# Residual, first norm, output projection and embedding gate with tokens on the partitions, and layer 1 begun by halves

## The chip, the cores and the metric

One of the eight cores of a Trainium2 chip runs the whole program. The time of a run is the time on the device in microseconds (us). Where a profile is quoted, it is one execution, recorded by the hardware profiler; its span reaches from the first to the last instruction.

## What is computed

Two layers of an encoder on 512 tokens of 1024 channels, all in float32. Each layer has a mixer and an MLP:

```python
for i in range(DEPTH):                                   # 2
    h = _mixer_sublayer(x, cos, sin, w_in[i], ...)       # two attentions, gated: (ga*ya + gb*yb) @ w_out
    x = _layer_norm(DEEPNORM_ALPHA * x + h, ln1_g[i], ln1_b[i])
    mlp = square(relu(x @ w_up[i])) @ w_down[i]          # 1024 -> 4096 -> 1024
    gate = sigmoid(x @ w_ple_gate[i] + b_ple_gate[i])
    ple = gate * (p[i] @ w_ple[i])                       # p[i]: 512 x 256
    x = _layer_norm(DEEPNORM_ALPHA * x + mlp + ple, ln2_g[i], ln2_b[i])
return x
```

## The kernel before, in words

**Number format.** Every operand of a matmul is split into a high part in TensorE's rounded float32 and a low part, the rest (`split`, L224: a cast on ScalarE (ACT), a subtraction on VectorE (DVE)). A product is then three matmuls: high x high, high x low, low x high (`mm3`, L269). The weights stand in memory in the order of use. `fetch` (L234) loads a set of eight 128x128 blocks (512 KB) by a DMA on SyncE's queue (SP), `prep` (L243) splits it, `ahead` and `weights` (L251, L262) keep a given number of sets in front of TensorE (PE); three buffers each for raw, high and low sets.

**Layout.** Channels lie on the partitions nearly everywhere: the activations are `X`, eight pairs of 128 channels by 512 tokens. A projection holds a block of weights still and streams 512 tokens past it. Only the MLP's second half (`Down`, L959) has tokens on the partitions; it uses a scheme of seven products in place of eight, with sums and differences of blocks.

**Order of a layer.** (1) The first projection `start` (keys, values, two queries; `linear_k_outer`, L283: four PSUM banks, input blocks in the outer loop), then attention, whose PE order is chosen by a small model (`Forecast`, L163), with gate projections as filling. (2) The second gates and branch projections give `M`, eight pairs (L1201 to L1215). (3) The residual `y` is put together as high + low of X on GpSimd (POOL, L1224). (4) The output projection goes block by block (`linear`), each block followed by `Norm.tile` (L854): residual added on DVE, squares on ACT, sums over blocks on POOL. Since the norm runs over partitions here, `begin` (L834) first subtracts an approximate mean (`shifted`, L824), and `finish` (L907) has TensorE make the sums over channels: 32 matmuls with one column (`moment`, L870), then statistics on DVE, then rows of mean and scale by transposes (`token_row`, L901). The embedding's matmuls (`ple_part`, L1177) fill in between. DVE and ACT then make the new X (`scaled`, L943, and L951) and the residual with bias. (5) The embedding gate: four blocks with k outer, four single ones; `embed` (L1237) adds gate times embedding to y. (6) The MLP. With its first two blocks the residual is turned to tokens on the partitions (`residual_turned`, L1250: 32 transposes on PE, copies on ACT). Four quarters, each with eight blocks `up` and seven products (`Down.product`, L1037; sums into y by `gather`, L1064). (7) The second norm, written out by hand for PE, DVE and ACT (L1328 on): batch statistics on DVE (`moments`, `statistics`), scaling (`scaled`, L1099), then `turned` (L1109) transposes back to channels in two halves of the tokens and applies scale and bias per channel. In layer 0 this gives the next X (`high`, `full`, `low`), with the next embedding half in between; then `start` of layer 1 follows. In layer 1 `store` (L1137) writes the transposed output in eight DMAs.

In a `manual_schedule` block the named engines keep the order of the text; elsewhere a planner sets the order of the engines.

Of the kernel before, what the change touches and what calls it, by code (L numbers as in the profile page):

```python
# [30 lines left out]
NEG = -3.0e38  # L31
LOOK = 2
# [10 lines left out]
def plan_layer(l):  # L43
# [35 lines left out]
    for t in range(KT):  # L79
        out.append(m_outer(("wo", t), "w_out", cols((t * P, P))))  # L80

    def ple(l, hh):
        return (("ple", l, hh), [("w_ple", l, [full[k]], cols(((hh * 4 + m) * P, P)))
                                 for m in range(4) for k in range(2)])

    if l == 0:
        out.append(ple(l, 0))
    out.append(ple(l, 1))
    gates = [cols((t * P, P)) for t in range(KT)]
    out += k_outer("pg0", "w_ple_gate", gates[:4])  # L90
    for t in range(4, KT):
        out.append(m_outer(("pg", t), "w_ple_gate", gates[t]))
# [108 lines left out]
def build(nc, tc, plan, down, xT, pT, wst, vec, sink, cst, outT):  # L201
# [3 lines left out]
    with ctx:  # L205
# [10 lines left out]
        rgap = rg.tile([P, 80], F32, name="rgap")  # L216
        nc.gpsimd.memset(rgap, 0.0)
        onec = cp.tile([P, 1], F32, name="onec")
        wgap = wp.tile([P, 96], F32, name="wgap", bufs=1)
        nc.gpsimd.memset(wgap, 0.0)  # L220
        nc.vector.memset(onec, 1.0 / D)
# [5 lines left out]


        offs = np.cumsum([0] + [len(t) * P * P for _, t in plan + down])
        down_at = {key: int(offs[len(plan) + n]) for n, (key, _) in enumerate(down)}  # L230
        ready, fetched = {}, {}
# [11 lines left out]
        def prep(c):  # L243
            st, n, cut = fetched.pop(c)
            hi = wp.tile([P, 1024], F32R, tag="whi", name=f"whi{c}")
            lo = wp.tile([P, 1024], F32R, tag="wlo", name=f"wlo{c}")
            for a in range(0, n, cut):
                split(hi[:, a:a + cut], lo[:, a:a + cut], st[:, a:a + cut])
            ready[c] = (hi, lo)
# [19 lines left out]
        def mm3(ps, w, i, x, start, stop):  # L269
            s = slice(i * P, (i + 1) * P)  # L270
            nc.tensor.matmul(ps, w[0][:, s], x[0], start=start, stop=False)  # L271
            nc.tensor.matmul(ps, w[0][:, s], x[1], start=False, stop=False)  # L272
            nc.tensor.matmul(ps, w[1][:, s], x[0], start=False, stop=stop)  # L273
# [20 lines left out]


# [13 lines left out]
        def attention_block(l, av, rp, vt, OA, OB):  # L309
# [371 lines left out]
            kps, vps, q0, q1 = linear_k_outer(l, "start", X, load_constants)  # L681
# [127 lines left out]
        class Norm:  # L809
            def __init__(self, mp, y, alpha, name):  # L810
                self.mp, self.y, self.alpha, self.name = mp, y, alpha, name

            def add(self, out, ps, y):
                if self.alpha == 1.0:
                    nc.vector.tensor_tensor(out, ps, y, ALU.add)
                else:
                    nc.vector.scalar_tensor_tensor(out, y, self.alpha, ps, ALU.mult, ALU.add)

            def shift(self, ps):
                zr = self.mp.tile([P, S], F32R, tag="zr", name="zr" + self.name, bufs=1)  # L820
                self.add(zr, ps, self.y[0])
                return zr

            def shifted(self, zr):  # L824
                ones_r = self.mp.tile([P, P], F32R, tag="ones", name="ones" + self.name, bufs=1)
                nc.vector.memset(ones_r.bitcast(F32), 1.0 / P)
                cb = bank("o", "cb" + self.name)
                nc.tensor.matmul(cb, ones_r, zr, start=True, stop=True)
                cs = self.mp.tile([P, S], F32, tag="shift", name="cs" + self.name, bufs=1)
                nc.scalar.activation(cs, cb, AF.Copy, scale=1.0 / self.alpha)  # L830
                for u in range(KT):
                    (nc.gpsimd if u else nc.vector).tensor_tensor(self.y[u], self.y[u], cs, ALU.subtract)

            def begin(self, keys, xs):  # L834
                with tc.manual_schedule(engines={PE}):
                    ws, pss = [], []
                    for n in range(2):
                        ws.append(weights(keys[n]))
                        pss.append(bank("mm", f"first{self.name}_{n}"))
                        for i in range(KT - 1):  # L840
                            mm3(pss[n], ws[n], i, xs[i], i == 0, False)
                    mm3(pss[0], ws[0], KT - 1, xs[KT - 1], False, True)
                    zr = self.shift(pss[0])
                    mm3(pss[1], ws[1], KT - 1, xs[KT - 1], False, True)
                    w = weights(keys[2])
                    ps = bank("mm", f"first{self.name}_2")
                    for i in range(KT):
                        if i == 2:
                            self.shifted(zr)
                        mm3(ps, w, i, xs[i], i == 0, i == KT - 1)  # L850
                for t, p in enumerate(pss + [ps]):
                    self.tile(t, p)
# [17 lines left out]
            def moment(self, dst, src):  # L870
                for j in range(dst.shape[-1]):
                    nc.tensor.matmul(dst[:, j:j + 1], src[:, j * P:(j + 1) * P], onec, start=True, stop=True)
# [532 lines left out]
```

## Time and profile before

| | us |
|---|---|
| median of 3 runs | 1574.93 (1572.06 to 1576.66) |
| profiled execution, its time | 1573.54 |
| its span | 1571.8 |
| its TensorE busy time | 1533.4 |
| its mean granted TensorE clock | 0.996 |

In the views a line such as L226 is one of the kernel above; PE, DVE, ACT, POOL and SP are TensorE, VectorE, ScalarE, GpSimd and SyncE; PEld is the loading of the operand that stands still. `128x512` is partitions by elements. Matmuls overlap: one of 512 columns is shown as 0.39 us long, but the next starts 0.227 us after it, so the distance of starts is their cost. A wait names the engine and line that came last. The rows follow with the prediction.

### The profile page before, as it was taken

To read this page: it belongs to the slowest core of one execution; us is meant where nothing else is said; L and a number is where in the kernel's file an instruction comes from. 1 tells how busy PE (TensorE), PEld (TensorE's weight loads), DVE (VectorE), ACT (ScalarE), POOL (GpSimd) and SP (SyncE) were. 2 spreads that over 40 slices of the span, in tenths; PEclk is the share of its full clock that TensorE was granted. 3 is DMA by queue.
4 is the path that set the end of the run, shared out by engine and by line. 5 is a ranking of instruction groups with operands and counts; after the bars stand their busy time and mean duration, and the time that the engine had idled before them with its cause. 6 is when DMAs were issued, how large, how long until landed. Compare 5 with 4: busy or idle time off the path is not lost.

```text
span 1571.8 us, 19688 instructions
## 1 busy us (share of the span) xinstructions
PE 1533.4 (98%) x7482; PEld 1254.0 (80%) x7482; DVE 1079.9 (69%) x1759; ACT 741.6 (47%) x1237; POOL 288.4 (18%) x208
## 2 busy tenths in 40 slices
PE   8999999999999999999899999999999999999997
PEld 6777888878888888888677778888887888888886
DVE  6878674454947777686868786744549476777867
ACT  4666554333644443434445665543336444434343
POOL 1010100157111111202000101101572111112020
PEclk9999999999999999999999999999999999999999
DMA  6212122232532414141132112223325324241401
GB/s 216 68 54 67 55 82 85 90 104 77 221 94 69 132 56 151 49 148 41 40 106 68 54 57 66 78 79 99 95 79 206 103 75 128 65 149 46 142 1 54
DMA packets 42736, 143.37 MB, mean 91 GB/s; under 512 B 5136, under 2 KB 7312, under 8 KB 42640
## 3 DMA queue, kind: packets, MB, share of 16 engines
q1 hardware_dynamic: 42064, 142.03, 28.4%
q8 instruction: 59, 0.97, 0.3%
q14 instruction: 37, 0.30, 0.1%
q10 hardware_dynamic: 576, 0.07, 0.0%
HBM read 139.98 MB, written 2.10 MB: 90 GB/s over the span
## 4 chain that ended last, share of the span: by engine, by line
PE 86%; DVE 8%; ACT 3%; issue 2%; DMA 1%; SPq 0%; ACTq 0%; DVEq 0%
PE dn L1051 16%; PE ps_up L273 7%; PE ps_up L272 7%; PE ps_up L271 7%; DVE wlo L226 2%; PE sa L399 1%; PE pta L377 1%; PE ps_start L271 1%; PE ps_start L272 1%; PE sb L399 1%; PE ps_start L273 1%; PE ya L271 1%; PE ya L273 1%; PE ya L272 1%; PE ps_pg L272 1%
## 5 line engine op out<-in xcount | busy, mean ns | idle before, releaser
L226 DVE TENSOR_TENSOR wlo<-wst,whi 128x1024 fp32r<-128x1024 f32 (+1 forms) x197 | 261.7, 1332 | 184.6 <-ACT whi L225 167.8
L225 ACT CAST whi<-wst 128x1024 fp32r<-128x1024 f32 (+1 forms) x197 | 202.3, 1029 | 352.8 <-PE ps_up L272 106.7
L1024 POOL TENSOR_TENSOR hr<-r 128x512 f32<-128x512 f32 x64 | 102.1, 1595 | 568.5 <-ACT r L1016 568.5
L271 PE MATMUL ps_up<-xhi,whi 128*128 128x512 f32 x480 | 186.9, 389 | 0.0
L273 PE MATMUL ps_up<-xhi,wlo 128*128 128x512 f32 x480 | 186.7, 389 | 0.0
L272 PE MATMUL ps_up<-xlo,whi 128*128 128x512 f32 x480 | 186.7, 389 | 0.0
L225 ACT CAST whi<-raw 128x1024 fp32r<-128x1024 f32 x56 | 58.0, 1052 | 101.4 <-PE ps_up L272 62.0
L272 PEld LDWEIGHTS ps_up<-xlo,whi 128*128 128x128 f32 x480 | 90.1, 188 | 18.8
L271 PEld LDWEIGHTS ps_up<-xhi,whi 128*128 128x128 f32 x480 | 90.1, 188 | 18.7
L273 PEld LDWEIGHTS ps_up<-xhi,wlo 128*128 128x128 f32 x480 | 90.1, 188 | 18.5
L225 ACT CAST dhi<-raw 128x1024 fp32r<-128x1024 f32 x56 | 58.8, 1052 | 82.8 <-PE dn L1051 59.5
L1070 DVE TENSOR_TENSOR yt<-yt,dn 128x512 f32<-128x512 f32 x96 | 65.3, 682 | 43.4 <-PE dn L1051 43.4
L1004 DVE TENSOR_TENSOR raw<-raw,raw 128x1024 f32<-128x1024 f32 x64 | 86.4, 1350 | 0.9 <-DMA raw<-wst 0.7
L226 DVE TENSOR_TENSOR wlo<-raw,whi 128x1024 fp32r<-128x1024 f32 x56 | 68.2, 1221 | 17.8 <-ACT whi L225 17.8
L226 DVE TENSOR_TENSOR dlo<-raw,dhi 128x1024 fp32r<-128x1024 f32 x56 | 68.2, 1220 | 5.1 <-ACT dhi L225 5.1
L336 POOL TENSOR_TENSOR sw_qb<-sw_qb,ct 128x512 f32<-128x512 f32 x12 | 18.4, 1536 | 181.9 <-DVE sw_qb L334 181.9
L1051 PE MATMUL dn<-whi,smh 128*128 128x512 f32 x128 | 50.1, 394 | 0.7 <-DVE yt L1070 0.7
L1051 PE MATMUL dn<-wlo,smh 128*128 128x512 f32 x128 | 50.6, 395 | 0.2
L1211 POOL TENSOR_TENSOR gate<-gate,gate 128x512 f32<-128x512 f32 x16 | 25.0, 1585 | 140.2 <-DVE gate L1210 140.2
L1051 PE MATMUL dn<-whi,sml 128*128 128x512 f32 x128 | 49.9, 390 | 0.0
L1051 PE MATMUL dn<-dhi,smh 128*128 128x512 f32 x128 | 49.9, 389 | 0.0
L1051 PE MATMUL dn<-dlo,smh 128*128 128x512 f32 x128 | 49.8, 389 | 0.0
(1015 smaller groups left out, 4048.0 us busy)
## 6 DMA issues: line engine op xcount, KB each, us to landing
wst<-wst SPq DMA_DIRECT2D x187, 512.0 KB, 3.6
raw<-wst SPq DMA_DIRECT2D x64, 512.0 KB, 4.4
wst<-wst SPq DMA_DIRECT2D x10, 256.0 KB, 2.7
xs<-xT SPq DMA_DIRECT2D x8, 256.0 KB, 4.7
outT<-nt SPq DMA_DIRECT2D x8, 256.0 KB, 2.2
ct<-cst SPq DMA_DIRECT2D x2, 960.0 KB, 8.0
pf<-pT SPq DMA_DIRECT2D x4, 256.0 KB, 4.0
pf<-pT SPq DMA_DIRECT2D x1, 512.0 KB, 3.5
```

What stands on the lines that cost most here:

```text
L225: nc.scalar.copy(hi, src)
L226: nc.vector.tensor_tensor(lo, src, hi.bitcast(F32), ALU.subtract)
L271: nc.tensor.matmul(ps, w[0][:, s], x[0], start=start, stop=False)
L272: nc.tensor.matmul(ps, w[0][:, s], x[1], start=False, stop=False)
L273: nc.tensor.matmul(ps, w[1][:, s], x[0], start=False, stop=stop)
L336: nc.gpsimd.tensor_tensor(sw, sw, cc["sin"], ALU.mult)
L399: nc.tensor.matmul(ss[r][:, col], q[a][rs, qs], k[b][rs, ks], start=n == 0, stop=n == 2)
L1004: nc.vector.tensor_tensor(to, to, other, ALU.add)
L1024: nc.gpsimd.tensor_tensor(h.rearrange("p s t -> p (s t)"), r, r, ALU.mult)
L1051: nc.tensor.matmul(ps[s], a[:, k, tok], w[b][:, cols], start=first and not (k or m), stop=k == 3 and m == 2, skip_group_check=True)
L1070: return nc.vector.tensor_tensor(to, to, ps, ALU.subtract if n in (2, 4, 5) else ALU.add)
L1211: nc.gpsimd.tensor_tensor(g, g, ga[t], ALU.add)
```

## The change

Residual, output projection, first norm and gate now have tokens on the partitions, four blocks of 128 tokens by 1024 channels, as the MLP's second half had already.

- The residual `y` is loaded by DMA: in layer 0 from a second copy of the input (`xN`), in layer 1 from a copy in device memory (`kept`) that layer 0 stores. Its former sum and the turning of the residual are gone.
- Matmuls of these projections hold tokens still and stream 512 columns of weights (`mm3t`). The output projection takes its first half of channels with the input blocks outer, its second half token block by token block; the gate likewise by halves and token blocks. 14 more buffers (seven pairs) for weight sets (`wb`).
- The norm (`Tokens`) uses batch statistics for both norms. ACT subtracts the mean, DVE multiplies by the token's scale and a row of per-channel scales loaded to all partitions (`row`); 16 transposes per half of the tokens turn the result, and bias and split are made out of PSUM (`parts`).
- A bias in the token layout is added by an accumulating DMA issued from GpSimd (`add_row`). For three operands (the next layer's embedding input, its first embedding weights, the first set of layer 1's `start`) the low part is made by two ACT operations and such a DMA (`split_later`).
- Layer 1's `start` runs its first two sets on 256 tokens, then the second half of the norm is turned, then the rest.
- The output is written with tokens on the partitions; no transposes at the end.

```diff
+        def split_later(hi, lo, src):
+            nc.scalar.copy(hi, src)
+            nc.scalar.activation(lo, hi.bitcast(F32), AF.Copy, scale=-1.0)
+            nc.gpsimd.dma_start(lo, src, accum_op=ALU.add)
...
+        def mm3t(ps, x, w, i, start, stop):
+            c = slice(i * 512, (i + 1) * 512)
+            nc.tensor.matmul(ps, x[0], w[0][:, c], start=start, stop=False)
+            nc.tensor.matmul(ps, x[0], w[1][:, c], start=False, stop=False)
+            nc.tensor.matmul(ps, x[1], w[0][:, c], start=False, stop=stop)
...
+        def start_by_halves(l, then):
...
+            for j in range(2):
+                ws.append(weights((l, ("start", j)), 1 - j))
+                part(j, slice(0, 256))
+            then()
+            for j in range(2):
+                part(j, slice(256, S))
+            for j in range(2, 4):
+                ws.append(weights((l, ("start", j)), 3 - j))
+                part(j, slice(0, S))
+            return pss
...
+        class Tokens:
...
+            def statistics(self, a):
...
+                nc.vector.tensor_scalar(m, self.mv[:, a:a + 2, 0], -1.0, None, ALU.mult)
+                nc.vector.tensor_scalar(v, self.mv[:, a:a + 2, 1], LN_EPS, None, ALU.add)
+                for i in range(2):
+                    nc.scalar.activation(self.y[a + i], self.y[a + i], AF.Identity, bias=m[:, i:i + 1])
...
+            def scaled(self, a, g, c=slice(0, D)):
+                x = self.y[a][:, c]
+                nc.vector.scalar_tensor_tensor(x, x, self.rs[a], g[:, c], ALU.mult, ALU.mult)
...
+            def parts(self, a, tps, ks, b):
+                c = slice(a * P, a * P + 256)
+                for j in ks:
+                    for k in (2 * j, 2 * j + 1):
+                        nc.scalar.activation(xhi[:, k, c], tps[k], AF.Identity, bias=b[:, k:k + 1])
+                    for k in (2 * j, 2 * j + 1):
+                        nc.vector.scalar_tensor_tensor(xlo[:, k, c], tps[k], b[:, k:k + 1], xhi[:, k, c].bitcast(F32),
+                                                       ALU.add, ALU.subtract)
...
+        def add_row(y, l, i):
+            nc.gpsimd.dma_start(y, rows[l, i].partition_broadcast(P), accum_op=ALU.add)
...
+            for a in range(4):
+                nc.sync.dma_start(y[a], kept[a] if l else xN[a])
+                if l:
+                    add_row(y[a], l - 1, 4)
...
+            def turned(a):
+                tps = tn.transposed(a, ("pt", "pt", "s", "s"))
+                tn.parts(a, tps, range(4), b1)
+                for i in range(2):
+                    add_row(y[a + i], l, 2)
...
+            def embed(a, h, ws):
...
+                nc.vector.tensor_tensor(t, ps, bg[:, c], ALU.add)
+                nc.scalar.activation(t, t, AF.Tanh, scale=0.5)
+                nc.vector.scalar_tensor_tensor(t, t, 1.0, ple[h, a], ALU.add, ALU.mult)
+                nc.vector.scalar_tensor_tensor(y[a][:, c], y[a][:, c], ALPHA, t, ALU.mult, ALU.add)
...
+                turned(0)
+                if not l:
+                    embedding(l, 0, PL, p0)
+                else:
+                    embedding(l, 1, PL, np1)
+                ws = [weights((l, ("pg0", j)), 3 - j) for j in range(4)]
+                embed(0, 0, ws)
+                embed(1, 0, ws)
+                turned(2)
+                if not l:
+                    embedding(l, 1, PL, np1)
...
+                embed(2, 0, ws)
+                embed(3, 0, ws)
...
             with tc.manual_schedule(engines={PE, DVE, ACT}):
                 dn.cut(q, 6, 0)
...
+                def fifth(s):
+                    tn.moments(2 + s, 1)
+                    if not s:
+                        tn.statistics(0)
+                        return
+                    if not last:
+                        ahead(at[0] + 1)
+                    tn.scaled(0, g2)
+                    tn.scaled(1, g2)
+
+                dn.product(q, 5, fifth)
                 if last:
+                    for a in range(2):
+                        add_row(y[a], l, 4)
+                        nc.sync.dma_start(out[a], y[a])
+                    dn.product(q, 6, lambda s: tn.moments(2 + s, 0))
+                    tn.statistics(2)
+                    for h, engine in enumerate((nc.gpsimd, nc.vector)):
+                        c = slice(h * 512, (h + 1) * 512)
+                        for a in (2, 3):
+                            tn.scaled(a, g2, c)
+                            engine.tensor_tensor(y[a][:, c], y[a][:, c], b2r[:, c], ALU.add)
+                            nc.sync.dma_start(out[a][:, c], y[a][:, c])
+                else:
...
+                    embedding(l + 1, 0, PL, p0, range(2))
+                    tp = tn.transposed(0, ("pt", "pt", "o", "s"))
+                    tn.parts(0, tp, (0,), b2)
+                    ahead(at[0] + 1)
+                    tn.parts(0, tp, (1,), b2)
+                    embedding(l + 1, 0, PL, p0, range(2, 4))
+                    tn.statistics(2)
+                    tn.scaled(2, g2)
+                    tn.scaled(3, g2)
+                    tn.parts(0, tp, (2, 3), b2)
+
+                    def second():
+                        tp = tn.transposed(2, ("pt", "pt", "o", "s"))
+                        tn.parts(2, tp, (0,), b2)
+                        ahead(at[0])
+                        tn.parts(2, tp, (1, 2, 3), b2)
+                        for a in range(2, 4):
+                            nc.sync.dma_start(kept[a], y[a])
+
+                    begun = start_by_halves(l + 1, second)
```

More of the change, by code (lines that the diff above doesn't have):

```diff
@@ L31 @@
 NEG = -3.0e38
+LATER = ((0, ("ple", 1, 0)), (1, ("start", 0)))
 LOOK = 2
@@ L78, in plan_layer, with ple @@
                                 for t in (2 * u, 2 * u + 1) for i in range(2)]))
[L79 to L92, printed above, removed]
+    blocks = [cols((t * P, P)) for t in range(KT)]
+    def ple(l, h):
+        return (("ple", l, h), [("w_ple", l, [full[k]], c) for k in range(2) for c in blocks[4 * h:4 * h + 4]])
+    for h in range(2):
+        out += k_outer(f"wo{h}", "w_out", blocks[4 * h:4 * h + 4])
+    out.append(ple(l, l))
+    out += k_outer("pg0", "w_ple_gate", blocks[:4])
+    if not l:
+        out.append(ple(l, 1))
+    out += k_outer("pg1", "w_ple_gate", blocks[4:])
     for q in range(FQ):
@@ L197, in give, with build @@
         f[f.index(1e9)] = until
-def build(nc, tc, plan, down, xT, pT, wst, vec, sink, cst, outT):
+def build(nc, tc, plan, down, xT, xN, pT, wst, vec, rows, sink, cst, out):
     ctx = ExitStack()
@@ L1099, in scaled @@
-            def scaled(self, a, own):
-                r, s = self.statistics(a)
-                for k in range(2):
-                    for i in range(2):
-                        x = self.y[a + i][:, k * 512:(k + 1) * 512]
-                        if 2 * k + i < own:
-                            nc.vector.tensor_scalar(x, x, r[:, i:i + 1], s[:, i:i + 1], ALU.mult, ALU.add)
-                        else:
-                            nc.scalar.activation(x, x, AF.Identity, bias=s[:, i:i + 1], scale=r[:, i:i + 1])
@@ new lines, in build, with projected @@
+            pf = np1.tile([P, 2, S], F32, tag="pf", name=f"pf{l}", bufs=1)
+            nc.sync.dma_start(pf, pT[l])
+            split(ph, pl, pf)
+            PL = [(ph[:, k], pl[:, k]) for k in range(2)]
+            bg, g1 = row(np1, l, 0, "bg"), row(np1, l, 1, "g1")
+            wb, wb_close = pool(f"wb{l}", "right")
+            held_sets.update({n: (wb, "b", 7) for n in ("wo1", "pg0", "pg1")})
+            tn = Tokens(np1, y, f"n1_{l}")
+            def projected(a, h, ps):
+                x = y[a][:, h * 512:(h + 1) * 512]
+                nc.vector.scalar_tensor_tensor(x, x, ALPHA, ps, ALU.mult, ALU.add)
+                tn.moments(a, h)
@@ L1398 @@
     args = [nc.dram_tensor(n, a.shape, mybir.dt.from_np(a.dtype), kind="ExternalInput").ap() for n, a in arrays.items()]
[L1399 removed]
+    args.append(nc.dram_tensor("out", (4, P, D), F32, kind="ExternalOutput").ap())
     with tile.TileContext(nc, schedule_with_timeline_sim=True) as tc:
```

472 lines of the change are left out of this document (147 added, 325 removed).

## Prediction

> **What bounds the kernel now.** I read the page first (span, busy time, chain of waits), then busy time by stretches cut where the change starts and stops, then the waits of TensorE, and last the timeline and the groups by line for durations.
>
> ```profile
> span 1571.8 us, 19688 instructions
> PE 1533.4 (98%) x7482; PEld 1254.0 (80%) x7482; DVE 1079.9 (69%) x1759; ACT 741.6 (47%) x1237; POOL 288.4 (18%) x208
> PE 86%; DVE 8%; ACT 3%; issue 2%; DMA 1%; SPq 0%; ACTq 0%; DVEq 0%
> ```
>
> TensorE is busy for 1533.4 of 1571.8 us and carries 86% of the chain. So an edit gains only where it takes work off TensorE or closes one of the gaps, 38.4 us in all. The next table shows how much of that lies where the change works (a row is one stretch: its limits and length, then the busy us of PE, PEld, DVE, ACT and POOL with their instructions, the granted clock, the DMA share and GB/s).
>
> ```profile
> 335.45:454.20 118.75, 117.64 (x555) 97.76 (x553) 76.61 (x90) 55.32 (x76) 58.35 (x38) 1.00 0.39 133
> 457.00:773.10 316.10, 314.97 (x1381) 258.16 (x1380) 230.62 (x283) 130.25 (x160) 47.89 (x30) 1.00 0.28 86
> 773.10:816.20 43.10, 35.70 (x153) 28.09 (x152) 27.08 (x58) 24.83 (x43) 0.96 (x1) 0.92 0.33 109
> 1122.50:1239.30 116.80, 113.01 (x531) 93.05 (x530) 76.10 (x89) 52.26 (x71) 57.88 (x38) 1.00 0.39 131
> 1557.30:1571.80 14.50, 5.94 (x33) 4.81 (x31) 6.61 (x22) 8.64 (x17) 0.00 (x0) 0.78 0.44 146
> ```
>
> The rows are, in order: layer 0 from its output projection through first norm, embedding gate and the turning of the residual; its MLP; the passage into layer 1 up to the end of the first projection; layer 1's own stretch of the first kind; and the tail behind the last matmul. The MLP has 1.1 us without work, and the change leaves it as it is. Of the four others, the passage is the worst: 7.4 us idle and a clock of 0.92.
>
> **What TensorE does there beside its matmuls.** A 128x512 matmul costs TensorE 0.227 us in a row of them: one product of the MLP, 24 of them, takes 5.45 us. The pieces of the chain give the extras of the first norm and of the residual's turning:
>
> ```profile
> 734.47 5.45 PE dn L1051 x24
> 379.68 0.79 PE m1n L872 x8
> 381.28 0.78 PE m2n L872 x8
> 384.25 0.79 PE m1n L872 x8
> 385.04 0.89 PE m2n L872 x8
> 385.93 0.49 PE Mn L904 x4
> 388.49 0.47 PE Rn L904 x4
> 445.44 1.75 PE yT L1254 x16
> 452.64 1.75 PE yT L1254 x16
> ```
>
> **Stretch 1 (layer 0).** It holds 192 matmuls of the output projection, 48 of the embedding, 192 of its gate and 48 of the MLP: 480 x 0.227 = 109.0 us of 118.75. The other 9.75 us are moments 3.25 (L872), rows of mean and scale 0.96 (L904), the shift's one matmul 0.23 (L828), the residual's transposes 3.5, and about 1.8 of waits and slow restarts. The change keeps all 480: operands only trade places (tokens stand still, weights stream), each still 128 rows by 512 columns. Moments, rows and shift go to VectorE's batch statistics and per-token scalars. The 32 residual transposes go, and 32 others come, which turn the normalised tokens for the next matmuls: again 3.5 us. That leaves 109.0 + 3.5 = 112.5. Both turnings have cover: the first is followed by the embedding's 24 matmuls (5.45 us), the second too; without it each would show some 2 us. I leave 0.6 for waits: 113.1, a gain of **5.6** (bounds 4 to 6.2).
>
> Waits of TensorE, longest in total (total us, times, longest):
>
> ```profile
> PE ps_pg L272 <- DVE xlo L951: 2.7, 2, 2.1
> PE xT L1115 <- DVE yt L1105: 2.1, 1, 2.1
> PE ple L271 <- ACT ph L225: 1.8, 1, 1.8
> PE ps_start L272 <- DVE xlo L1135: 1.5, 1, 1.5
> PE ps_start L271 <- ACT xhi L1124: 1.3, 1, 1.3
> PE ple L271 <- ACT ple L1189: 1.3, 1, 1.3
> PE ple L272 <- DVE pl L226: 1.1, 1, 1.1
> PE ps_('wo', 3)_3384 L271 <- DVE y L817: 1.1, 1, 1.1
> ```
>
> **Stretch 4 (layer 1).** One embedding half less: 456 x 0.227 = 103.5, plus 3.5 of new transposes is 107.0 of 116.80. The wait of the gate for `xlo` (2.7, first row) goes with the old norm. What is late next: after the second turning no embedding stands in between here, and the gate's matmuls wait for `xhi` and `xlo`. Each pair of blocks costs VectorE two operations on 128x256, TensorE uses it for 6 matmuls:
>
> ```profile
> L1032 DVE SCALAR_TENSOR_TENSOR sr<-sr,hr 128x256 f32<-128x256 f32 x32 | 13.6, 425 | 1.1
> L1124 ACT ACTIVATE xhi<-xT,vraw 128x256 fp32r<-128x256 f32 x16 | 8.3, 578 | 3.3 <-DVE nt L1126 3.3
> ```
>
> Two at 0.43 (0.85 us) are faster than 6 x 0.227 = 1.36 us, so only the first pair is waited for: two 0.58 on ScalarE and one 0.43 on VectorE, and ahead of them in VectorE's queue the previous gate block's bias and its wait for the tanh. I take 2.5 us, between nothing and the 5.45 that layer 0 hides it under. 109.5: a gain of **7.3** (4.4 to 9.8).
>
> **Stretch 3 (the passage).** 24 embedding matmuls, 32 transposes, 96 matmuls of the first projection: 120 x 0.227 + 3.5 = 30.7 us of work in 43.1. The lost 12.4 us are the six waits on xT, ple and ps_start above, 9.1 less the 2.1 on `yt` (L1105), which is the tail's, and matmuls at half rate after each:
>
> ```profile
> 781.77 0.63 PE L271 MATMUL ple<-ph,whi 128*128 128x512 f32 x1
> 782.20 0.63 PE L272 MATMUL ple<-pl,whi 128*128 128x512 f32 x1
> ```
>
> 0.43 us apart instead of 0.227. The change works against all of it: embedding operands are split before the products end; two embedding blocks run ahead of the first turning and two after; half the projection's first 48 matmuls run on the first 256 tokens while the second half is normalised. Cutting 48 matmuls into 96 of 256 columns costs TensorE between nothing and 48 x 0.227 = 10.9 us; the nearest row has 256 columns:
>
> ```profile
> 78.38 0.28 PE L403 MATMUL oa<-ptha,vvva 128*128 128x256 f32 x1
> 78.49 0.28 PE L404 MATMUL oa<-ptla,vvva 128*64 128x256 f32 x1
> ```
>
> 0.11 us apart, half of 0.227, so I take 0.2 us for all. New on the path is VectorE, which now scales two whole token blocks in front of product 6's sums (durations in the groups):
>
> ```profile
> 1557.51 0.70 DVE yt L1070
> L1004 DVE TENSOR_TENSOR raw<-raw,raw 128x1024 f32<-128x1024 f32 x64 | 86.4, 1350 | 0.9 <-DMA raw<-wst 0.7
> 1552.79 0.69 DVE L1077 BATCH_NORM_STATS2 nst<-yt 128x6 f32<-128x512 f32 x1
> 1555.68 0.16 DVE L1096 SCALAR_TENSOR_TENSOR nsm<-nmv,nsm 128x2 f32<-128x2 f32 x1
> ```
>
> Call E the time of the last sum (1557.51 in layer 1; layer 0 is alike). Product 5's first half is ready at E-8.2, halves being 2.72 apart. VectorE from there: sum 0.7, moments and statistics 3.05 (1552.79 to 1555.84), sum and moments 1.4, two scalings of 128x1024 at 1.35: E-0.35, just before TensorE ends product 6. TensorE then has 12 embedding matmuls (2.7), 16 transposes (1.75), 12 more (2.7): busy to E+7.2. VectorE: two sums with moments 2.8 (E+2.4), then the first `xlo`, one weight split (1.35), statistics 2.4, scalings 2.7, and three more pairs at 0.85: near E+14. TensorE's two half-parts, 48 x 0.115 = 5.5, end at E+12.7; the second turning follows scaled tokens at about E+13, and about 1.5 us pass till its `xlo`. Allowing 3 us for all waits: 30.7 + 0.2 + 3 = 33.9, a gain of **9.2** (3 to 12.2). SP carries new stores of the kept residual, which wait for the scalings; behind them stand the last weight sets of the projection and the constants, which TensorE needs 10 us later and which land in 3.6 and 8.0 us in this trace; covered.
>
> **The tail.** Rows for its last pieces:
>
> ```profile
> 1565.69 1.19 DVE L1126 TENSOR_SCALAR nt<-xT,vraw 128x256 f32<-128x256 f32 x2 [0.31 <-ACT nt L1124]
> L1024 POOL TENSOR_TENSOR hr<-r 128x512 f32<-128x512 f32 x64 | 102.1, 1595 | 568.5 <-ACT r L1016 568.5
> outT<-nt SPq DMA_DIRECT2D x8, 256.0 KB, 2.2
> wst<-wst SPq DMA_DIRECT2D x187, 512.0 KB, 3.6
> ct<-cst SPq DMA_DIRECT2D x2, 960.0 KB, 8.0
> ```
>
> Before, the last result is ready at 1566.88, E+9.4, after 32 transposes. After, none are left, but the two scalings are in front: VectorE reaches the sums at E-0.35, ends the last one at E+1.8, statistics at E+4.85, then four half scalings and two additions at 0.69: E+9.0. GpSimd's two additions (1.6 each) run beside them from E+5.5: E+8.7. The tail gains nothing. For six stores on one queue, behind a wait, I add **1.0** (-1 to +6).
>
> **The accumulating DMAs.** Bias rows and the low halves of three operands are added by DMAs issued from GpSimd. The trace has none. Nearest row: 512 KB in 3.6 us; I price them at that, and at more in the rival. At 3.6 they are covered: start's low half has about 9 us (E-1.9 to E+7.2), the bias rows have two gate blocks of time. In layer 1 four of them stand on GpSimd's queue ahead of the gates' sums (L1211), which TensorE first uses in the output projection, eight gates later. SP's new loads at that place (residual, rows) and the MLP's first raw weights, which now wait for the norm's memory, meet the same order of queue as in the MLP's later quarters, where 1.1 us in 316.10 are without work; I price them at nothing, at most 2 us.
>
> [...]
>
> **Sum.** -5.6 - 7.3 - 9.2 + 1.0 = -21.1 us. The profiled execution took 1573.54 us (span 1571.8 and 1.74 around it): 1552.4. The median of the runs shown is 1574.93, 1.4 higher: **1554 us**.
>
> **Rivals.**
>
> *The waits come back at the passage.* VectorE is the one engine through which everything there goes, and my count has it finish within a microsecond of TensorE's need. If its queue slips, TensorE waits again and falls to half rate as in the two rows at 782. With 9 of the 12.4 us lost again, 5 in layer 1 and 3 in the tail: -5.6 - 4.8 - 3.2 + 3 = -10.6, 1564; with a worse first norm, 1567. For it: VectorE's queue is strictly ordered there. Against: 43 us hold 27 us of VectorE work.
>
> *Slower: the accumulating DMAs are slow and run one after another.* Price each at T. The first output bias is issued when its block is scaled, E-1.7, so two end at about E-1.7+2T and are needed by E+9; the second pair of bias rows in each layer is needed 14.5 us after its turning, the first pair 17.5; VectorE waits in order, and with it the banks and TensorE. At T = 10: tail +9, turnings 2 x (5.5 + 2.5), start +1: 26 us lost, 1580. It decides from T of about 9.5; at 8 the change still gains 13. Against: the largest transfer here, 960 KB, lands in 8.0 us.
>
> *No effect.* TensorE's extras removed are 2 x 4.4 us by the rows above whatever else happens; no change needs as much lost elsewhere.
>
> **How the numbers follow.** Forecast 0.75, waits back 0.17, slow DMAs 0.08. The bounds of the four terms at their best, -6.2 - 9.8 - 12.2 - 1 = -29, give 1546; the first rival's end gives the top, 1567. The slower rival is left out. A measurement of this kernel tells about 0.3%, 4.7 us. Faster by more: 0.87; within: 0.05, the edge of both rivals; slower: 0.08.
>
> **What would show it.** L872, L904 and the residual's transposes gone; stretch 1 about 113 us, stretch 4 about 109.5, the passage about 34 with a clock above 0.95; no `xT` transposes at the end and a tail of 14 to 16 us. Wrong if a wait on a GpSimd DMA stands high among VectorE's or TensorE's waits, if 256-column matmuls lie 0.2 us apart, or if the MLP stretch grows from 316 us.

## The result, and the profile after

The changed kernel took 1546.6 us (median, 1546.11 to 1546.96), the kernel before 1574.93: a ratio of 0.9826, 95% interval 0.9814 to 0.9838 (the two medians divide to 0.982; beside the later runs the kernel before took 1572.8 to 1573.5 us). The profiled execution took 1546.11 us (span 1544.3), against 1573.54 (span 1571.8). From the page of the changed kernel:

```profile
span 1544.3 us, 19518 instructions
PE 1512.5 (98%) x7416; PEld 1241.6 (80%) x7416; DVE 1091.1 (71%) x1809; ACT 714.9 (46%) x1186; POOL 201.3 (13%) x159
PE 89%; DVE 6%; ACT 2%; DMA 2%; issue 1%; SPq 0%; ACTq 0%; DVEq 0%
```

TensorE is busy for 20.9 us less, and the span is 27.5 shorter: the rest are gaps that closed. Where, the busy time by stretches shows (limits and length, busy us of PE, PEld, DVE, ACT and POOL, granted clock, DMA share, GB/s). First the changed kernel:

```profile
335.76:448.15 112.39, 112.39 (x514) 93.52 (x513) 71.37 (x115) 43.29 (x62) 8.80 (x7) 1.00 0.51 155
448.15:766.32 318.17, 317.32 (x1393) 260.63 (x1392) 246.01 (x295) 142.46 (x171) 52.15 (x34) 1.00 0.32 96
766.32:798.01 31.69, 31.67 (x202) 28.49 (x201) 20.83 (x46) 16.09 (x29) 1.02 (x1) 1.00 0.66 201
...
1104.25:1212.36 108.11, 107.23 (x490) 88.91 (x488) 69.95 (x114) 40.14 (x57) 8.66 (x7) 1.00 0.53 156
1212.36:1530.79 318.43, 317.60 (x1393) 260.34 (x1391) 246.12 (x295) 136.03 (x165) 50.61 (x33) 1.00 0.27 85
1530.79:1544.30 13.51, 0.15 (x1) 0.00 (x0) 10.04 (x23) 2.19 (x2) 4.04 (x3) 0.67 0.81 233
```

Then the kernel before, cut at the same instructions (its other rows stand in the prediction, to within 0.1 us):

```profile
454.15:773.10 318.95, 317.82 (x1395) 260.52 (x1394) 232.50 (x286) 132.87 (x166) 49.39 (x31) 1.00 0.28 86
1239.21:1557.31 318.10, 317.66 (x1395) 260.51 (x1393) 233.77 (x288) 132.90 (x166) 49.37 (x31) 1.00 0.26 80
```

| stretch | before | after | measured | forecast |
|---|---|---|---|---|
| 1: layer 0, projection to second up block | 118.70 | 112.39 | -6.3 | -5.6 |
| its MLP | 318.95 | 318.17 | -0.8 | 0 |
| 3: the passage | 43.11 | 31.69 | -11.4 | -9.2 |
| 4: layer 1, projection to second up block | 116.73 | 108.11 | -8.6 | -7.3 |
| its MLP | 318.10 | 318.43 | +0.3 | 0 |
| tail | 14.49 | 13.51 | -1.0 | +1.0 |

The two attention stretches, left out here, differ by 0.3 and 0.05 us. All of the gain lies where the change works, and in the passage the granted clock went from 0.92 to 1.00. TensorE waits for one thing there still in this profile, in layer 1 behind the second turning (total us, times, longest):

```profile
PE pg L282 <- DVE xlo L901: 0.9, 1, 0.9
```

### The profile page after: what moved, and what is told of

The parts are those of the page before. It is cut to its first block, busy times and chain, and to the rows that moved or that the text cites. A ratio compares the mean times of both kernels' runs of the same rounds, so it can differ in the third digit from the quotient of the medians.

```text
span 1544.3 us, 19518 instructions
## 1 busy us (share of the span) xinstructions
PE 1512.5 (98%) x7416; PEld 1241.6 (80%) x7416; DVE 1091.1 (71%) x1809; ACT 714.9 (46%) x1186; POOL 201.3 (13%) x159
## 4 chain that ended last, share of the span: by engine, by line
PE 89%; DVE 6%; ACT 2%; DMA 2%; issue 1%; SPq 0%; ACTq 0%; DVEq 0%
PE dn L1004 17%; PE ps_up L275 8%; PE ps_up L274 8%; PE ps_up L276 8%; PE wo L281 2%; PE wo L282 2%; PE wo L280 2%; PE pg L282 2%; PE pg L281 2%; PE pg L280 2%; DVE wlo L223 1%; PE sa L433 1%; PE sb L433 1%; PE pta L411 1%; PE ps_start L274 1%
## 5 line engine op out<-in xcount | busy, mean ns | idle before, releaser
L223 DVE TENSOR_TENSOR wlo<-wst,whi 128x1024 fp32r<-128x1024 f32 (+1 forms) x171 | 220.2, 1291 | 149.5 <-ACT whi L222 144.8
L222 ACT CAST whi<-wst 128x1024 fp32r<-128x1024 f32 (+1 forms) x171 | 175.5, 1026 | 295.2 <-PE ps_up L275 115.5
L274 PE MATMUL ps_up<-xhi,whi 128*128 128x512 f32 x512 | 199.2, 389 | 0.0
L275 PE MATMUL ps_up<-xlo,whi 128*128 128x512 f32 x512 | 199.2, 389 | 0.0
L276 PE MATMUL ps_up<-xhi,wlo 128*128 128x512 f32 x512 | 199.2, 389 | 0.0
L274 PEld LDWEIGHTS ps_up<-xhi,whi 128*128 128x128 f32 x512 | 96.1, 188 | 20.0
L276 PEld LDWEIGHTS ps_up<-xhi,wlo 128*128 128x128 f32 x512 | 96.1, 188 | 20.0
L275 PEld LDWEIGHTS ps_up<-xlo,whi 128*128 128x128 f32 x512 | 96.1, 188 | 19.9
L1023 DVE TENSOR_TENSOR y<-y,dn 128x512 f32<-128x512 f32 x96 | 65.1, 682 | 38.7 <-PE dn L1004 38.7
L282 PE MATMUL pg<-bhi,xlo 128*128 128x512 f32 x128 | 49.9, 390 | 0.9 <-DVE xlo L901 0.9
L280 PE MATMUL pg<-bhi,xhi 128*128 128x512 f32 x128 | 49.9, 390 | 0.0
```

What stands on the lines that cost most here:

```text
L222: nc.scalar.copy(hi, src)
L223: nc.vector.tensor_tensor(lo, src, hi.bitcast(F32), ALU.subtract)
L280: nc.tensor.matmul(ps, x[0], w[0][:, c], start=start, stop=False)
L282: nc.tensor.matmul(ps, x[1], w[0][:, c], start=False, stop=stop)
L1023: return nc.vector.tensor_tensor(to, to, ps, ALU.subtract if n in (2, 4, 5) else ALU.add)
```

## The experiments

The theory after the result: each stretch ahead of the tail came down to TensorE's own work, since VectorE's chain arrives in time nearly everywhere. The passage needs its parts together: light operands, and halves that give TensorE work while the second half is normalised. Rivals: one part alone does it; the cover has much room; the accumulating DMAs are what limits. Ratios are to the kernel before, with intervals; they are to be held against 0.9826. Where the times are too close, the stretches decide.

**1. The projection not begun by halves.**

```diff
-            for j in range(2):
-                ws.append(weights((l, ("start", j)), 1 - j))
-                part(j, slice(0, 256))
             then()
-            for j in range(2):
-                part(j, slice(256, S))
-            for j in range(2, 4):
-                ws.append(weights((l, ("start", j)), 3 - j))
+            for j in range(4):
+                ws.append(weights((l, ("start", j)), 3 - j if j > 1 else 1 - j))
                 part(j, slice(0, S))
```

> The changed kernel, but layer 1's first projection is not begun by halves: both halves of the tokens are turned first, then the projection runs at full width. Theory (the halves are what hides the second half's norm): in the changed kernel TensorE is through with the embedding at 773.56 and VectorE ends the second pair's scaling at 778.40, so TensorE now idles 4.9 us ahead of the second turning and about 1 us behind it, and restarts slowly after both: the passage grows from 31.7 to 38 to 41 us, total 1552.5 to 1555.5. Rival (the passage was closed by cheaper operands, with low halves straight from the turned bank and weights split by ScalarE and a DMA, and the halves add nothing): passage 32 to 33, total 1546 to 1548.

Measured: 1553.33 us, ratio 0.9874 (0.9861 to 0.9888). Its passage, and TensorE's timeline in it (start, length, engine, line, idle before and who ended it):

```profile
767.32:805.23 37.91, 33.63 (x154) 28.01 (x153) 21.05 (x46) 16.42 (x29) 1.02 (x1) 0.91 0.54 168
```

```profile
774.33 0.39 PE L282 MATMUL ple<-whi,pl 128*128 128x512 f32 x1
778.34 0.45 PE L885 MATMUL xTn<-ident,y 128*128 128x128 f32 x1 [3.62 <-DVE y L877]
779.45 3.46 PE L885 MATMUL xTn<-ident,y 128*128 128x128 f32 x15 [0.66 <-DVE y L877]
782.56 0.78 PE L274 MATMUL ps_start<-xhi,whi 128*128 128x512 f32 x1
783.13 0.63 PE L275 MATMUL ps_start<-xlo,whi 128*128 128x512 f32 x1
784.36 0.40 PE L275 MATMUL ps_start<-xlo,whi 128*128 128x512 f32 x1
```

The passage grew by 6.2 us, to just under the theory's 38. 4.3 of them are waits, the rest is what follows them: 15 transposes take 3.46 us where 16 took 1.91, the first matmuls lie 0.43 to 0.57 us apart, and the clock of the stretch is 0.91. Against the kernel before (43.11) the rest of the change without the halves still brings 5.2 us.

**2. Halves alone, on the kernel before.** The kernel before with `start_by_halves` of the change, and the second half's operands made behind its first two sets; all else as before.

```diff
-                second = dn.turned(1, ("s", "s", "pt", "pt"))
                 for k in range(KT):
                     if k > 3:
                         first.high(k, g2, b2)
                         first.full(k, g2, b2, nc.scalar)
-                    second.high(k, g2, b2)
                     first.low(k)
-                    second.full(k, g2, b2, nc.vector)
-                    second.low(k)
+                def second():
+                    tp = dn.turned(1, ("pt", "pt", "o", "s"))
+                    for k in range(KT):
+                        tp.high(k, g2, b2)
+                        tp.full(k, g2, b2, nc.vector)
+                        tp.low(k)
...
+                begun = start_by_halves(l + 1, second)
```

> The kernel before with one part of the change alone: layer 1's first projection begun by halves of the tokens, everything else (channels on the partitions, scale and bias behind the turning) as before. Theory (halves and the lighter VectorE work are both needed): the work of 5.5 us that TensorE gets ahead of the second turning covers only a part of the 12.4 us lost, since VectorE and ScalarE still have 27 and 25 us of work in the passage: passage 43.1 to 37 to 40, total 1569 to 1572. Rival (the order is all): passage 32 to 33, total 1563 to 1564. Second rival (VectorE's and ScalarE's longer chains leave the first half as late as the whole was): no gain, passage 42 to 45.

Measured: 1574.68 us, ratio 1.0012 (1.0003 to 1.0021), passage 44.8. It had a fault of its own: the fourth bank of the first turning made TensorE wait 4.5 us for a sum. So it was tried again with the old bank:

```diff
-                first = dn.turned(0, ("pt", "pt", "o", "s"))
+                first = dn.turned(0, ("pt", "pt", "o", "mm"))
```

> As the kernel before with the projection begun by halves, but the fourth bank of the first turning is taken from the same group as in the kernel before, since in the first try TensorE waited 4.5 us for VectorE's sum in the other bank. Theory (halves and the lighter VectorE work are both needed): the 4.5 us go, the 3.1 us for the low half of the first weight set stay, passage 44.8 to about 40, so 3 us less than the kernel before. Rival (halves alone bring the whole gain once no bank is in the way): passage 32 to 34. Second rival (halves are worth nothing with the old chain: ScalarE and VectorE end the second half as late as before): passage 43 or more.

Measured: 1575.91 us, ratio 1.0022 (1.0012 to 1.0031). The theory's 40 us did not come; the passage and its longest wait:

```profile
773.12:818.60 45.48, 37.48 (x202) 32.12 (x201) 27.18 (x58) 24.93 (x43) 0.97 (x1) 0.89 0.31 102
```

```profile
791.11 0.58 PE L272 MATMUL ps_start<-xlo,whi 128*128 128x256 f32 x1 [3.10 <-DVE xlo L1160]
799.65 1.91 PE L1140 MATMUL xT<-ident,yt 128*128 128x128 f32 x16
```

The second turning (799.65) shows no wait, so there was nothing for the halves to hide: in this kernel TensorE waits for the operands of the first half (ScalarE's two passes over each block, 0.57 and 0.56 us, then VectorE), and behind that wait its 48 half-width matmuls run slowly, 8.5 us instead of 5.8. The halves are worth 6.2 us in the changed kernel; without it they cost 2.4. What makes them pay is the rest of the change; which part of it, no run here separates beyond run 3.

**3. The low halves by VectorE again.**

```diff
-LATER = ((0, ("ple", 1, 0)), (1, ("start", 0)))
+LATER = ()
...
-                    split_later(ph, pl, pf)
+                    split(ph, pl, pf)
```

> The changed kernel with the low parts of the three operands (next embedding input, its weights, the first weight set of the projection) made by VectorE's subtraction again instead of a second ScalarE operation and an accumulating DMA. VectorE gets 3 operations of 1.23 us more around the passage. Theory (VectorE reaches the second turning with only 0.9 us to spare, 778.40 for 779.32): one or two of them stand ahead of the second pair's scaling, so TensorE waits 0.5 to 3 us more, total 1547 to 1550. Rival (VectorE is idle for 10.9 of 31.7 us in the passage and takes the work in its gaps): no change, 1546 to 1547.

Measured: 1547.5 us, ratio 0.9837 (0.9824 to 0.9851), which the time can't tell from the changed kernel. The passage is 31.67, as before the edit. From the first up block of layer 0 to the passage it took 329.97 instead of 329.02 us, and TensorE's waits for VectorE's sums were 2.3 instead of 1.5 us. But in the other experiments on the changed kernel, none of which edits this piece, it took 329.0 to 329.7 us, and the waits were 2.2 us in run 9. So the rival was right for the passage; in front of it the three operations are worth at most 1 us, and that they are worth anything is not shown.

**4. Twice as many accumulating DMAs.**

```diff
             nc.gpsimd.dma_start(y, rows[l, i].partition_broadcast(P), accum_op=ALU.add)
+            nc.gpsimd.dma_start(y, zero[0].partition_broadcast(P), accum_op=ALU.add)
```

> The changed kernel with every accumulating bias DMA followed by a second one of the same size that adds a row of zeros: 28 instead of 14. Theory (they are covered, and two in flight share the DMA engines rather than waiting for each other's 7.8 us): nothing in the turnings, since the pairs have 14 us or more; only in the tail, where the DMA engines are 81% busy for 13.5 us, two more of about 2.8 us of all engines each push the stores back, plus 1 to 4 us: total 1547 to 1550. Rival (each takes its 7.8 us in turn, so a price of 15.6 us per row, beyond the 9.5 us from which the prediction's slower rival decides): TensorE or VectorE waits for them in both layers and the tail, total 1560 or more.

Measured: 1551.48 us, ratio 0.9863 (0.9849 to 0.9876). The projections' stretches and the passage (31.68) are the same to 0.3 us, and the tail is 18.1 instead of 13.5. Its timeline:

```profile
1530.19 0.89 POOL L910 DMA_DIRECT2D y<-rows  x1 [34.74 <-DVE y L882]
1535.43 0.87 POOL L911 DMA_DIRECT2D y<-zero  x1 [3.17 <-DMA y<-rows]
1538.32 0.87 POOL L911 DMA_DIRECT2D y<-zero  x1 [2.03 <-DMA y<-rows]
1538.75 3.50 DVE L882 SCALAR_TENSOR_TENSOR y<-y,nsmn,row 128x512 f32<-128x512 f32 x1
1538.88 2.81 POOL L1270 TENSOR_TENSOR y<-y,row 128x512 f32<-128x512 f32 x2
```

The second DMA of a block waits for the first, as the rows show, and the chains of two blocks run beside each other (begun at 1530.19 and 1531.39). A block's two took some 16 us (medians 8.3 and 7.5; in the tail alone 5.7 and 5.0), beyond the 9.5 of the prediction's slower rival. In the body even that is covered. In the tail it isn't, by 4.6 us, somewhat over the theory's 4. The first two stores wait for the doubled rows: they start 9.1 us after TensorE's last matmul does instead of 3.8, and the last four stand behind them on SP's queue. GpSimd's own additions also stand behind its second issue, from 1538.88, and one of VectorE's scalings took 3.50 us beside them instead of 0.74; still, VectorE's last result came only 0.8 us later.

**5. Layer 0's cover taken away.** Layer 1 stays as it was.

```diff
-                turned(0)
                 if not l:
                     embedding(l, 0, PL, p0)
+                    turned(0)
...
-                turned(2)
                 if not l:
                     embedding(l, 1, PL, np1)
+                turned(2)
```

> The changed kernel with layer 0's two embedding pieces moved ahead of the two turnings of the first norm, so that the gate's matmuls follow each turning directly, as they do in layer 1 behind the second one. Theory (by layer 1's row: 0.88 us of wait for the low half, matmuls a little slow behind it): about 1 us for each turning, layer 0's stretch from 112.4 to 114.4, total 1548.5. Rival, the prediction's word for it (some 2 us each): 116.4, total 1550.5. Second rival (the cover is worth its whole 5.45 us since VectorE is busy with the second pair's norm): over 120, total 1555 or more.

Measured: 1551.14 us, ratio 0.9861 (0.9847 to 0.9874). From the first matmul of the projection to the first up block 105.5 us instead of 101.54:

```profile
385.43 1.91 PE L890 MATMUL xTn<-ident,y 128*128 128x128 f32 x16
388.03 0.50 PE L280 MATMUL pg<-bhi,xhi 128*128 128x512 f32 x1 [0.70 <-ACT xhi L899]
390.21 0.50 PE L282 MATMUL pg<-bhi,xlo 128*128 128x512 f32 x1 [1.45 <-DVE xlo L901]
...
406.22 1.91 PE L890 MATMUL xTn<-ident,y 128*128 128x128 f32 x16
408.38 0.50 PE L280 MATMUL pg<-bhi,xhi 128*128 128x512 f32 x1 [0.25 <-ACT xhi L899]
409.66 0.50 PE L282 MATMUL pg<-bhi,xlo 128*128 128x512 f32 x1 [0.55 <-DVE xlo L901]
```

4.0 us for two turnings: 2.7 for the first (2.60 from its start to the gate's first matmul where 1.66 is usual, 2.18 from there to the third where 0.45 is), 1.3 for the second (2.16 and 1.28). Layer 1's row (0.88) was too small a guide; the prediction's "some 2 us" held for the sum.

**6. VectorE later in the passage.**

```diff
+                    idle = qp.tile([P, D], F32, name="idle", tag="raw011", bufs=1)
+                    for n in range(2):
+                        nc.vector.tensor_tensor(idle, y[0], y[1], ALU.add)
                     tn.statistics(2)
```

> The changed kernel with two additions of 128x1024 (1.35 us each, into memory that nothing reads) put into VectorE's queue just ahead of the second pair's statistics in the passage. Theory (VectorE's chain to the second turning is what comes next: it ends its scaling at 778.40, TensorE wants to turn at 779.32, so 0.9 us are to spare): 2.6 us more make TensorE wait 1.7 us, and what follows the turning is late by as much: passage 31.7 to 33.4, or to 34 and over if the matmuls restart slowly, total 1548.3 to 1550. Rival (VectorE idles 10.9 us in the passage, so that its order leaves it room): passage 31.7 to 32, total 1546.6.

Measured: 1548.53 us, ratio 0.984 (0.9827 to 0.9853); the passage 33.31 instead of 31.69:

```profile
766.51:799.82 33.31, 32.04 (x201) 28.43 (x200) 23.18 (x48) 16.20 (x29) 1.01 (x1) 1.00 0.60 192
```

```profile
779.93 0.30 PE L890 MATMUL xTn<-ident,y 128*128 128x128 f32 x1 [0.30 <-DVE y L882]
781.03 1.50 PE L890 MATMUL xTn<-ident,y 128*128 128x128 f32 x11 [0.81 <-DVE y L882]
```

2.5 us more on VectorE, 1.6 us more in the passage: 0.9 us were to spare, as read from the trace. VectorE's order is the next limit, though it is idle a third of the time (busy 20.83 of 31.69 us in the changed kernel's passage). In run 3 the added operations stood ahead of the passage in its queue.

**7. Layer 1's cover divided**, and the tail's additions of run 8.

```diff
                 else:
-                    embedding(l, 1, PL, np1)
+                    embedding(l, 1, PL, np1, range(2))
...
                 turned(2)
-                if not l:
-                    embedding(l, 1, PL, np1)
+                embedding(l, 1, PL, np1, range(2 * l, 4))
```

> The changed kernel with layer 1's embedding divided, two blocks behind the first turning of the first norm and two behind the second (all four stood behind the first), and the last four bias additions all on VectorE. Theory (layer 1's one wait is the 0.88 us behind the second turning, and 12 matmuls, 2.7 us, cover either turning, since without cover the waits in layer 0 were 2.15 and 0.80 us): stretch 4 from 108.1 to 107.1, tail 13.0 instead of 13.5, together 1.5 us: 1545.1, which the time can hardly tell from the changed kernel. Rival (the first turning needs all of its 5.45 us of cover, since VectorE has the second pair's norm to do): the wait moves to the first turning, stretch 4 at 108 to 110, and only the tail gains.

Measured: 1551.11 us, ratio 0.9856 (0.9842 to 0.9869). Slower than the changed kernel, against the theory:

```profile
1164.18 0.39 PE L282 MATMUL pg<-bhi,xlo 128*128 128x512 f32 x1
1167.27 0.30 PE L890 MATMUL xTn<-ident,y 128*128 128x128 f32 x1 [2.70 <-DVE y L882]
1168.37 3.45 PE L890 MATMUL xTn<-ident,y 128*128 128x128 f32 x15 [0.80 <-DVE y L882]
1171.48 0.56 PE L280 MATMUL ple<-whi,ph 128*128 128x512 f32 x1
```

From the projection to the first up block layer 1 took 101.56 us instead of 97.23. The wait of 0.88 behind the second turning is not there, and one of 3.5 stands ahead of that turning: the blocks taken from the first piece had also covered the second pair's scaling. The rival named the right work, but at the wrong turning. That the 0.88 went by the edit is not shown: it is nothing in runs 3 and 9 and 0.2 in run 8, which leave this part as it is, and there layer 1 took 96.4, 96.1 and 96.6 us to the same block. The tail was 13.06, as expected.

**8. The last four additions on VectorE.**

```diff
-                    for h, engine in enumerate((nc.gpsimd, nc.vector)):
+                    for h, engine in enumerate((nc.vector, nc.vector)):
```

> The changed kernel with the last four bias additions all on VectorE instead of two on GpSimd and two on VectorE. In the changed kernel the last additions took VectorE 1.63 and 0.69 us, and three scalings 3.08 instead of 3 times 0.74, while GpSimd's two took 3.37. Theory (VectorE stands still while GpSimd works on the same memory): VectorE now needs 4 times 0.74 and 4 times 0.69, 5.7 us from the end of the statistics, 6.1 before: the tail ends 0.4 us earlier, 13.1 instead of 13.5. Rival (the two engines run freely beside each other and the long rows are waits for something else): two additions more on VectorE, tail 1.4 us later, 14.9.

Measured: 1546.49 us, ratio 0.9829 (0.9816 to 0.9843); tail 13.03 instead of 13.51. VectorE in the changed kernel's tail, with GpSimd beside it:

```profile
1535.23 3.08 DVE L882 SCALAR_TENSOR_TENSOR y<-y,nsmn,row 128x512 f32<-128x512 f32 x3
1536.07 3.37 POOL L1269 TENSOR_TENSOR y<-y,row 128x512 f32<-128x512 f32 x2 [4.61 <-DVE y L882]
1538.35 1.63 DVE L1269 TENSOR_TENSOR y<-y,row 128x512 f32<-128x512 f32 x1
1539.90 0.74 DVE L882 SCALAR_TENSOR_TENSOR y<-y,nsmn,row 128x512 f32<-128x512 f32 x1
1540.68 0.69 DVE L1269 TENSOR_TENSOR y<-y,row 128x512 f32<-128x512 f32 x1
```

and alone, in the experiment (the first and the last of eight):

```profile
1535.01 0.75 DVE L882 SCALAR_TENSOR_TENSOR y<-y,nsmn,row 128x512 f32<-128x512 f32 x1
...
1539.96 0.69 DVE L1269 TENSOR_TENSOR y<-y,row 128x512 f32<-128x512 f32 x1
```

Six operations beside GpSimd took 6.14 us, eight alone 5.64: help that costs more than it gives. It is 0.5 us in the profile and too little for the time. No run was measurably faster than the changed kernel.

**9. Packets of 1 KB.** The output is laid out as `(4, 4, P, 256)`.

```diff
-                            nc.sync.dma_start(out[a][:, c], y[a][:, c])
+                            nc.sync.dma_start(out[a][2 * h:2 * h + 2].rearrange("q p x -> p q x"),
+                                              y[a][:, c].rearrange("p (q x) -> p q x", q=2))
```

> The changed kernel with the output laid out in rows of 256 channels, so that every stored packet is 1 KB as in the kernel before, instead of 2 or 4 KB. Theory (the tail came out 2 us shorter than forecast since the last store of 256 KB landed in 2.0 instead of 4.0 us, and that by its packets: before, 856 of 857 packets behind the last result were under 2 KB and a trickle of 8 to 31 GB/s followed for 1.5 us): the last stores land up to 2 us later, tail 15 to 15.5. Rival (the old end was late since eight stores stood close together): tail unchanged, 13.5.

Measured: 1547.05 us, ratio 0.9835 (0.982 to 0.985), tail 13.84: 0.3 us, not 2. The theory fell. What the 2 us were, run 2 shows by accident, since its tail is the code of the kernel before. The transfer rate from the last result to the end, in 40 slices, first in the kernel before (4.92 us), then in run 2's second try (3.44 us):

```profile
GB/s 291 291 375 358 325 341 291 500 366 275 358 291 350 325 308 308 84 8 8 17 17 25 25 25 25 25 25 25 17 0 0 0 0 0 0 0 0 0 0 0
```

```profile
GB/s 333 345 274 321 369 381 346 357 286 298 357 393 381 310 357 346 334 322 345 357 381 345 333 333 250 48 0 0 0 0 0 0 0 0 0 0 0 0 0 0
```

The trickle of 8 to 25 GB/s for 1.5 us stands in one of three profiles of this code: the old tail is 12.9 to 13.0 us in both tries of run 2, not 14.5. So it does not come with the code each time; what brought it stays open.

**10. The first norm's bias by VectorE.**

```diff
                 for i in range(2):
-                    add_row(y[a + i], l, 2)
+                    nc.vector.tensor_tensor(y[a + i], y[a + i], b1r, ALU.add)
```

> The changed kernel with the first norm's bias added to the residual by VectorE (four additions of 128x1024 in each layer, right behind the operands of each turning, from a row loaded to all partitions) instead of by eight accumulating DMAs; the other six stay. Theory (the DMAs were covered and VectorE is not the bound there: from the first turning to the MLP of layer 0 it is busy 32.3 of 57.3 us): 2.7 us more VectorE work behind each turning are mostly absorbed, at most 1 us per turning where the gate's first sums stand behind them: total 1546.5 to 1549. Rival (VectorE's queue behind the turnings has no room, and that is what the DMAs were for): each turning costs about 2 us, total 1553 or more.

Measured: 1549.14 us, ratio 0.985 (0.9837 to 0.9863). To the first up block layer 0 took 101.5 us, as without the edit, layer 1 98.3 instead of 97.2, since there no embedding covers the second turning (TensorE's longest wait for `xlo` is 1.4 instead of 0.9). Among the runs that leave this part alone layer 1 took 96.1 to 97.2 us, so the eight DMAs spare some 1 to 2 us by the stretches, 2.5 by the medians. Neither TensorE nor VectorE shows a wait for them in the changed kernel; only the output's first two stores do.

## Why the prediction was right, point by point

The forecast was 1554, the result 1546.6: right in sign and mechanism, with the gain under-sized by about 7 us, 0.6 us inside the range. By the profile the forecast was 1552.4, and the profiled execution took 1546.11; most of the rest is the step from one execution to the median, put at 1.4 us and 0.5 after the change. The failing terms are sizes, above all the tail and the allowances for waits.

- **Stretch 1**, 113.1 forecast, 112.39 measured, with TensorE busy for all of it. The 0.6 us for waits were not needed. Both turnings have cover, and run 5 gives its price, 4.0 us for two.
- **Stretch 4**, 109.5 forecast, 108.11 measured. The late operand was named rightly (`xlo`, the previous block's gate operations ahead of it in VectorE's queue); it was put at 2.5 us and cost 1.1 (0.88 of it as a listed wait) in this profile, and nothing in those of runs 3 and 9. Just ahead of these operations VectorE had stood 1.78 us for the high part of a weight set here, and 0.92 in run 9. ScalarE's four 128x256 took 1.55 us together, 0.39 each, not 0.58.
- **Stretch 3**, 33.9 forecast, 31.69 measured; the bare work had been put at 30.9, the halves' 0.2 in it. The 3 us for waits were mostly not needed: VectorE ended the second pair at 778.40, 0.9 us ahead of the turning, where the count had it about level with it (its scalings took 1.23 us instead of 1.35, a part of that), and the first `xlo` held up the matmuls behind the turning by some 0.4 us, not 1.5. The half-width matmuls cost 0.6 us, not 0.2: 48 of them took 5.76 us, 0.120 apart.

```profile
773.56 0.28 PE L274 MATMUL ps_start<-xhi,whi 128*128 128x256 f32 x1
775.92 2.48 DVE L882 SCALAR_TENSOR_TENSOR y<-y,nsmn,row 128x1024 f32<-128x1024 f32 x2
779.32 1.91 PE L890 MATMUL xTn<-ident,y 128*128 128x128 f32 x16
780.98 0.36 PE L274 MATMUL ps_start<-xhi,whi 128*128 128x256 f32 x1
781.37 0.39 PE L275 MATMUL ps_start<-xlo,whi 128*128 128x256 f32 x1
```

- **The tail**, +1.0 forecast, -1.0 measured. Two steps failed, in opposite directions. VectorE was to be done at E+9.0 and ended at E+10.4 (E, when the last sum can start, is 1530.99 here): its statistics were 0.6 us early, but its six last operations took 6.1 us beside GpSimd instead of 4.2 (run 8). That made the tail longer by 1.4. The stores made it shorter by 3.4: from the last result to the end the forecast left 6.3 us (4.9 as before, 0.4 by which the result was to come earlier, and the 1.0 added), and 2.9 passed. Of the 3.4, 1.5 is the yardstick, since the profile on which the old tail was priced holds the trickle of run 9, and 1.0 the allowance for six stores. Against the 12.9 to 13.0 of the other two profiles the new tail costs 0.5 to 0.6: the forecast's sign, and the -1.0 of the table is the old profile's trickle. The 13.5 us lie below the 14 to 16 that were named as a sign.
- **The accumulating DMAs** were priced at 3.6 us and took 7.8 (in the tail 5.6). The price was wrong and did not matter, since all of them are covered and they overlap: two issued 1.2 us apart in the tail took 5.6 each, not 11.2 in turn. The slower rival needed both, a price beyond 9.5 and one after another. What makes an accumulating DMA take longer than 3.6 us is not shown, nor that the adding is what costs: a plain load of such a row to all partitions, on SP's queue, took 9.4 us.

```profile
y<-rows POOLq DMA_DIRECT2D x14, 512.0 KB, 7.8
row<-rows SPq DMA_DIRECT2D x7, 512.0 KB, 9.4
```

- **Waits back at the passage** was the near miss: run 6 puts the point from which it begins at 0.9 us of VectorE time. In that run 1.6 us of VectorE time beyond that point made the passage 1.6 us longer; where two waits of TensorE near each other came to 4.3 us (run 1) and 3.5 us (run 7), the stretch grew by 6.2 and 4.3 us. That there were "matmuls at half rate after each" wait, as the prediction has it, is too much: in the kernel before, matmuls were at half rate from 780.2 to 783.5 and from 793.9 to 797.3, and at their usual distance behind the wait of 1.30 at 786.2.
- **The MLP** at 0: -0.8 and +0.3, of the size of the scatter told in run 3, not explained further.

## What to carry to other kernels

Cut the trace where the edit starts and stops and count TensorE's bare work in each piece: here that alone was within 0.1 to 1.1 us of the result, closer than with allowances for waits. A reordering that gives TensorE work during a wait is worth something only if that wait is the one it meets: halves were worth 6 us beside the rest of the change and nothing alone. And before a term is priced on one profiled execution's tail, hold it against a second profile of the same code.

## What the runs showed of the hardware

- Behind gaps on TensorE of 0.88 us (changed kernel), 1.45 (run 5) and 1.30 (the kernel before) the first matmul came 0.33 to 0.34 us ahead of the next, and the others lay at their usual 0.23. Behind 3.62 and 0.66 us (run 1) and 2.70 and 0.80 (run 7) 15 transposes took 3.46 and 3.45 us, where 16 took 1.91, and matmuls lay at their usual distance again 6.0 and 4.6 us after the first instruction behind the longer gap. In the kernel before, two gaps with a single matmul between them, 1.84 and 1.14 us, were followed 1 us later by matmuls 0.43 us apart, for 3.3 us, and two of 1.29 and 1.50 us, with two matmuls between them, 0.8 us later, for 3.4 us. From which length on a gap is followed by half rate is not shown.

```profile
777.48 0.49 PE L271 MATMUL ple<-ph,whi 128*128 128x512 f32 x1 [1.84 <-ACT ph L225]
779.12 0.50 PE L272 MATMUL ple<-pl,whi 128*128 128x512 f32 x1 [1.14 <-DVE pl L226]
```

- VectorE's operations of 128x512 took longer beside GpSimd's: one addition 1.63 us beside GpSimd's two in the changed kernel and 0.69 alone (run 8), one scaling 3.50 in run 4 and 0.74 alone (run 8). GpSimd's two additions took 3.37 us in the changed kernel and 2.81 in run 4, beside the scaling of 3.50. Why is not shown.
- An accumulating DMA of 512 KB from a broadcast row took 4.8 to 14.4 us to land, 7.8 in the median, in the changed kernel. The medians there for plain loads of that size go from 3.6 (weight sets) to 8.1 (embedding input) where the source is not a broadcast row, and are 9.4 where it is. The accumulating DMAs from a tile, of the same size, took 5.5 (weights) and 4.5 us (embedding input).
